# Merging the first loads of x in a matmul with bias and residual, and casting one tile on GpSimd

## The chip, the cores and the metric

The kernel runs on one core of one Trainium2 chip. The metric is device time in microseconds (us) of that core, lower being better. A core has five engines that run side by side[...]: PE (matmul, with PEld for its weight loads), DVE (VectorE), ACT (ScalarE), POOL (GpSimd) and SP, whose queue issues nearly all DMAs here. The profile also tells the share of the full TensorE clock that was granted at each moment (PEclk).

## The reference

```python
# x: (16, 512, 1024) f32, weight: (1024, 768) f32, bias: (768,) f32, residual: (16, 512, 768) f32
def reference(x, weight, bias, residual):
    return (np.matmul(x, weight) + bias + residual).astype(np.float32)
```

Flattened, x is 8192 rows of 1024 values and the output 8192 rows of 768.

## The kernel before, in words

**Tiling.** The 8192 rows are cut into 8 superblocks S of 1024 rows; partition p of a superblock holds 8 consecutive rows, so a superblock is `[128, J=8, 1024]`, and a tile t (64 in all) is the slice j = t % 8. A tile of x is 512 KB in f32. The contraction of 1024 is 8 steps of 128 (`steps`, c in 0..3 and e in 0..1); the output's 768 columns are two chunks, 512 and 256.

**What happens to a tile.** `cast(t)` converts x to bf16 into `xb[t]` (ring of 4). `transp(t)` views pairs of bf16 as f32, transposes four 128x128 blocks on PE into the PSUM tile `pt`, and DVE copies them to `xt[t]`. `mms(t, i)` runs the two chunks of one contraction step; 16 matmuls make a tile. `finish(t)` on DVE adds bias (tiles below 24) or the residual (later ones) to the PSUM result `po`, and `pool_add(t)` on POOL adds the rest. SP stores the result rows, which lie in the buffer that the residual was loaded to.

**Order.** Everything inside `keep_in_program_order` stays, on each engine, in the order in which the source issues it; nothing is planned by costs. SP's queue holds all loads and stores except the bias row, which ACT issues. The DMAs' completion semaphores are eight in rotation, so a DMA is issued only when the eighth one before it has landed.

**The head**, which the change touches, is written out by hand. SP issues, from first to last: tiles 0 and 1 of x as two DMAs (16 partitions, then the other 112), tile 2, the four blocks of weights `load_w(0..3)` of 768 KB each, then tile 3, tiles 4 and 5, tiles 6 and 7, and after these residual and x in turn. PE runs twelve dummy matmuls on a zeroed tile (`keep_warm(12)`), which keep it busy while nothing has landed, then the transposes of tiles 0 and 1, three more dummies, the transpose of tile 2, and a small matmul that spreads the bias row over the partitions (L193). Then the main matmuls start: for each weight block c, tiles 0, 1 and 2 in turn (`HEAD` = 3). DVE casts tile 0, ACT tiles 1 and 2; ACT and DVE cast the weights, half each, as the blocks land. From tile 3 on, one loop runs a tile per turn: the cast of tile t + 2 on ACT, sixteen matmuls with the transposes of tile t + 1 between them, `finish(t - 1)`. A buffer of x (two in a ring) is loaded again when all eight casts that read it are done.

The lines of the profile named below: L66 loads of x, L77 of weights, L74 of the residual; L89 the cast of x; L97 the transposes; L101 the copy to `xt`; L106 the main matmuls; L173 the dummies; L179 and L181 the casts of the weights; L193 and L201 the bias; L123 POOL's add.

Of the kernel before, what the change touches and what calls it, by code (L numbers as in the profile page):

```python
# [10 lines left out]
P = 128  # L11
J = 8
# [9 lines left out]
def kernel(  # L22
# [8 lines left out]
    nc = tc.nc  # L31
# [11 lines left out]
    x_d = x2d.rearrange("(S p j) k -> S p j k", p=P, j=J)  # L43
# [8 lines left out]
    def ring(pool, name, i, n, shape, dt):  # L52
        return pool.tile(shape, dt, name=name, tag=f"{name}{i % n}", bufs=1)
# [4 lines left out]
    x_sb, ro, xb, xt, po, tmp = {}, {}, {}, {}, {}, {}  # L58
    K_ = tc.keep_in_program_order


    def load_x(S, j0=0, j1=J, p0=0, p1=P):
        if S < n_s:
            if j0 == 0 and p0 == 0:
                x_sb[S] = ring(sb, "x_tile", S, X_BUFS, [P, J, K], FP32)
            K_(nc.sync.dma_start(  # L66
                out=x_sb[S][p0:p1, j0:j1, :], in_=x_d[S, p0:p1, j0:j1, :]
            ))

    def load_res(S, j0=0, j1=J):  # L70
        if S < n_s:
            if j0 == 0:
                ro[S] = ring(sb, "ro", S, RO_BUFS, [P, J, N], FP32)
            K_(nc.sync.dma_start(out=ro[S][:, j0:j1, :], in_=res_d[S, :, j0:j1, :]))  # L74

    def load_w(c):
        K_(nc.sync.dma_start(out=w_st[:, c, :, :], in_=w_d[:, c, :, :]))  # L77
# [7 lines left out]
    def cast(t, engine="act"):  # L85
        if t < n_t:
            xb[t] = ring(sb, "xb", t, 4, [P, K], BF16)
            copy = nc.scalar.copy if engine == "act" else nc.vector.tensor_copy
            K_(copy(out=xb[t], in_=x_sb[t // J][:, t % J, :]))  # L89

    def transp(t):
        if t < n_t:

            pt = ring(ps, "pt", t, 2, [P, n_c, P], FP32)
            pairs = xb[t][:, :].bitcast(FP32)
            for c in range(n_c):
                K_(nc.tensor.transpose(  # L97
                    out=pt[:, c, :], in_=pairs[:, c * P:(c + 1) * P], identity=ident
                ))
            xt[t] = ring(sb, "xt", t, 4, [P, n_c, P], FP32)  # L100
            K_(nc.vector.tensor_copy(out=xt[t], in_=pt))  # L101
# [37 lines left out]
    w_st = ring(sb, "ro", RO_BUFS - 1, RO_BUFS, [P, n_c, 2, N], FP32)  # L139
    w_sb = const.tile([P, n_c, 2, N], BF16, name="w_sb")  # L140

    load_x(0, 0, 2, 0, 16)
    load_x(0, 0, 2, 16, P)
    load_x(0, 2, 3)
    load_w(0)
    load_w(1)
    load_w(2)
    load_w(3)
    load_x(0, 3, 4)
    load_x(0, 4, 6)  # L150
    load_x(0, 6, 8)
    load_res(0, 0, 4)
    load_x(1, 0, 4)
    load_res(0, 4, 8)
# [16 lines left out]
    def keep_warm(n):  # L171
        for _ in range(n):
            K_(nc.tensor.matmul(  # L173
                warm_ps[:, 0:512], lhsT=warm[:, 0:P], rhs=warm, start=True, stop=True
            ))
# [5 lines left out]
            K_(nc.vector.tensor_copy(out=w_sb[:, c, e, :], in_=w_st[:, c, e, :]))  # L181


    keep_warm(12)
    cast(0, "dve")
    cast(1)
    transp(0)
    transp(1)
    keep_warm(3)
    cast(2)  # L190
    transp(2)
    for n0, nl in chunks:
        K_(nc.tensor.matmul(  # L193
# [23 lines left out]
    for t in range(HEAD, n_t):  # L217
        cast(t + 2)
        S, j = divmod(t, J)
# [30 lines left out]
    t, S = n_t - 1, n_s - 1  # L250
# [36 lines left out]
```

## Time and profile before

| | |
|---|---|
| median of 3 runs | 212.18 us (212.13 to 212.57) |
| the profiled execution | 212.57 us, of which the span from first to last instruction is 210.8 us and 1.8 us lie around it |
| PE busy | 201.7 us, 96% of the span |
| POOL, DVE, ACT busy | 115.7, 104.9 and 68.3 us |
| DMA | 87.23 MB, mean 414 GB/s |
| mean granted TensorE clock | 0.990 |

The page sums up one execution; the rows quoted below come from it and from four views of the same trace: the chain of work that ended last, in order of time; the timeline of an engine; the busy times and granted clock by stretch; and the DMA rates. In the chain, a piece is what the next piece waited for, and an engine's pieces follow each other without a gap. A matmul's modelled duration overlaps the next one's, so spacing between starts tells more than durations do.

### The profile page before, as it was taken

What the parts mean: (1) busy time and instruction counts of PE and PEld (TensorE: products, weight loads), DVE (VectorE), ACT (ScalarE), POOL (GpSimd) and SP (SyncE); (2) the same over time, 40 slices, a digit from 0 to 9 for tenths busy, and PEclk for the clock granted to TensorE, in tenths of its full rate; (3) what the DMA queues carried; (4) which work ended last, traced back from release to release, by engine and by line L of the source; (5) the groups of instructions that cost most, each with busy time, mean ns of one, the idle gap of its engine ahead of it and who ended that gap; (6) DMA issues with size and microseconds to landing.
All of it is one profiled execution on the core that took longest, in us unless ns stands there. A gap on an engine that the chain in (4) does not pass through costs nothing.

```text
span 210.8 us, 3154 instructions
## 1 busy us (share of the span) xinstructions
PE 201.7 (96%) x1274; PEld 131.8 (63%) x1299; DVE 104.9 (50%) x139; ACT 68.3 (32%) x68; POOL 115.7 (55%) x71
## 2 busy tenths in 40 slices
PE   7599999999999999999999999999999999999992
PEld 2366666666666666666666666666666666666651
DVE  0364554455445544554455455445544554455652
ACT  2443507240723142331333133321532333231000
POOL 2000077918865565799779901995059910699000
PEclk9889999999999999999999999999999999999999
DMA  6999999999999999999999999999999999999984
GB/s 170 373 414 426 443 403 443 454 395 438 432 454 421 420 438 404 463 431 412 428 443 431 424 415 429 452 426 426 438 423 432 442 417 423 434 438 421 423 373 182
DMA packets 5648, 87.23 MB, mean 414 GB/s; under 512 B 641, under 2 KB 769, under 8 KB 1922
## 3 DMA queue, kind: packets, MB, share of 16 engines
q1 hardware_dynamic: 5632, 87.03, 97.8%
q8 instruction: 10, 0.16, 0.3%
q14 instruction: 4, 0.03, 0.0%
q10 hardware_dynamic: 2, 0.00, 0.0%
HBM read 61.87 MB, written 25.17 MB: 413 GB/s over the span
## 4 chain that ended last, share of the span: by engine, by line
PE 93%; DMA 3%; DVE 1%; issue 1%; SPq 0%; DVEq 0%
PE po L106 78%; PE pt L97 14%; DMA x_tile<-in_x_dram 3%; PE po L193 1%; PE po L173 1%; DVE xb L89 0%; DVE xt L101 0%; DVE ro L133 0%; SPq L66 0%; DVEq L89 0%
## 5 line engine op out<-in xcount | busy, mean ns | idle before, releaser
L106 PE MATMUL po<-w_sb,xt 128*128 128x512 bf16 (+1 forms) x999 | 175.4, 324 | 1.4
L106 PEld LDWEIGHTS <-xt 128*128 128x128 bf16 x1024 | 100.1, 98 | 59.5 <-DVE xt L101 0.5
L89 ACT CAST xb<-x_tile 128x1024 bf16<-128x1024 f32 x62 | 63.5, 1045 | 117.5 <-PE pt L97 67.1
L123 POOL TENSOR_TENSOR ro<-ro,bias_sb 128x768 f32<-128x768 f32 x40 | 71.2, 1817 | 34.3 <-DMA ro<-in_residual_dram 23.0
L101 DVE COPY xt<-pt 128x512 f32<-128x512 f32 x64 | 44.3, 692 | 88.8 <-PE pt L97 88.7
L123 POOL TENSOR_TENSOR ro<-ro,tmp 128x768 f32<-128x768 f32 x24 | 43.2, 1817 | 44.5 <-DVE xt L101 25.6
L97 PE MATMUL pt<-ident,xb 128*128 128x128 f32 x256 | 39.3, 278 | 2.4 <-DVE xb L89 2.4
L133 DVE TENSOR_TENSOR ro<-po,ro 128x768 f32<-128x768 f32 (+2 forms) x41 | 38.0, 929 | 2.9 <-PE po L106 2.8
L97 PEld LDWEIGHTS pt<-ident,xb 128*128 128x128 f32 x256 | 30.8, 144 | 10.5 <-issue 3.3
L131 DVE TENSOR_TENSOR tmp<-po,bias_sb 128x768 f32<-128x768 f32 x24 | 22.8, 948 | 1.9 <-PE po L106 1.9
L173 PE MATMUL po<-warm 128*128 128x512 bf16 x15 | 6.2, 586 | 1.2 <-DVE warm L159 1.2
L89 DVE CAST xb<-x_tile 128x1024 bf16<-128x1024 f32 x2 | 1.4, 694 | 6.9 <-DMA x_tile<-in_x_dram 6.9
L173 PEld LDWEIGHTS <-warm 128*128 128x128 bf16 x15 | 2.0, 142 | 4.1 <-issue 2.8
L179 ACT CAST w_sb<-ro 128x768 bf16<-128x768 f32 x4 | 3.3, 832 | 4.0 <-DMA ro<-in_weight_dram 4.0
L181 DVE CAST w_sb<-ro 128x768 bf16<-128x768 f32 x4 | 2.1, 553 | 0.8 <-DMA ro<-in_weight_dram 0.8
L164 ACT ACT_TABLE_LOAD x1 | 1.3, 1283 | 2.0 <-POOL ident masks.py:199 2.0
L193 PE MATMUL po<-tmp 128*128 128x512 f32 (+1 forms) x4 | 1.5, 500 | 0.0
L193 PEld LDWEIGHTS po<-tmp 128*128 128x128 f32 x4 | 0.8, 240 | 0.5 <-issue 0.5
L201 DVE COPY bias_sb<-po 128x768 f32<-128x768 f32 x1 | 1.0, 958 | 0.1
L137 POOL MEMSET tmp<- 128x768 f32 x1 | 0.7, 737 | 0.3 <-POOLq L271 0.3
L159 DVE MEMSET warm<- 128x256 uint32 x1 | 0.3, 272 | 0.9 <-PEq L271 0.9
masks.py:199 POOL TENSOR_SCALAR_AFFINE_SELECT ident<-ident 128x128 f32<-128x128 f32 x1 | 0.3, 292 | 0.1
(8 smaller groups left out, 1.0 us busy)
## 6 DMA issues: line engine op xcount, KB each, us to landing
ro<-in_residual_dram SPq DMA_DIRECT2D x7, 3072.0 KB, 18.2
out_dram<-ro SPq DMA_DIRECT2D x7, 3072.0 KB, 24.0
x_tile<-in_x_dram SPq DMA_DIRECT2D x5, 4096.0 KB, 28.8
x_tile<-in_x_dram SPq DMA_DIRECT2D x4, 2048.0 KB, 26.5
ro<-in_weight_dram SPq DMA_DIRECT2D x4, 768.0 KB, 10.1
ro<-in_residual_dram SPq DMA_DIRECT2D x2, 1536.0 KB, 21.2
x_tile<-in_x_dram SPq DMA_DIRECT2D x2, 1024.0 KB, 15.0
out_dram<-ro SPq DMA_DIRECT2D x1, 1536.0 KB, 9.9
```

Of the source, the lines that this page charges most:

```text
L89: K_(copy(out=xb[t], in_=x_sb[t // J][:, t % J, :]))
L97: K_(nc.tensor.transpose(out=pt[:, c, :], in_=pairs[:, c * P:(c + 1) * P], identity=ident))
L101: K_(nc.vector.tensor_copy(out=xt[t], in_=pt))
L106: K_(nc.tensor.matmul(po[t][:, n0:n0 + nl], lhsT=both[:, e, :], rhs=w_sb[:, c, e, n0:n0 + nl], start=(i == 0), stop=(i == len(steps) - 1),))
L123: K_(nc.gpsimd.tensor_add(out=r, in0=r, in1=tmp[t] if t < EARLY else bias_sb))
L131: K_(nc.vector.tensor_add(out=tmp[t], in0=p, in1=bias_sb))
L133: K_(nc.vector.tensor_add(out=row(t, n0, nl), in0=p, in1=row(t, n0, nl)))
L164: K_(nc.scalar.copy(out=warm_a, in_=warm_a))
L173: K_(nc.tensor.matmul(warm_ps[:, 0:512], lhsT=warm[:, 0:P], rhs=warm, start=True, stop=True))
L179: K_(nc.scalar.copy(out=w_sb[:, c, e, :], in_=w_st[:, c, e, :]))
L181: K_(nc.vector.tensor_copy(out=w_sb[:, c, e, :], in_=w_st[:, c, e, :]))
L193: K_(nc.tensor.matmul(bias_ps[:, n0:n0 + nl], lhsT=ones, rhs=bias_row[:, n0:n0 + nl], start=True, stop=True,))
```

## The change

The first DMA of x takes all three tiles of the head, 1536 KB over 128 partitions; the loads after the weights take two tiles and three. Six DMAs of x become three. The cast of tile 2 moves from ACT to POOL. Two dummy matmuls move from between the transposes of tiles 1 and 2 to the stretch before the first transpose: 12 and 3 become 14 and 1.

```diff
-    def load_x(S, j0=0, j1=J, p0=0, p1=P):
+    def load_x(S, j0=0, j1=J):
         if S < n_s:
-            if j0 == 0 and p0 == 0:
+            if j0 == 0:
                 x_sb[S] = ring(sb, "x_tile", S, X_BUFS, [P, J, K], FP32)
-            K_(nc.sync.dma_start(
-                out=x_sb[S][p0:p1, j0:j1, :], in_=x_d[S, p0:p1, j0:j1, :]
-            ))
+            K_(nc.sync.dma_start(out=x_sb[S][:, j0:j1, :], in_=x_d[S, :, j0:j1, :]))
...
-            copy = nc.scalar.copy if engine == "act" else nc.vector.tensor_copy
+            copy = {
+                "act": nc.scalar.copy, "dve": nc.vector.tensor_copy,
+                "pool": nc.gpsimd.tensor_copy,
+            }[engine]
...
-    load_x(0, 0, 2, 0, 16)
-    load_x(0, 0, 2, 16, P)
-    load_x(0, 2, 3)
+    load_x(0, 0, 3)
     load_w(0)
     load_w(1)
     load_w(2)
     load_w(3)
-    load_x(0, 3, 4)
-    load_x(0, 4, 6)
-    load_x(0, 6, 8)
+    load_x(0, 3, 5)
+    load_x(0, 5, 8)
...
-    keep_warm(12)
+    keep_warm(14)
     cast(0, "dve")
     cast(1)
     transp(0)
     transp(1)
-    keep_warm(3)
-    cast(2)
+    keep_warm(1)
+    cast(2, "pool")
     transp(2)
```

## The prediction

> **What bounds the kernel now.** I read the chain of waits first, by engine for the whole page and then in order of time for the first 26 us, where all edits lie.
>
> ```profile
> PE 93%; DMA 3%; DVE 1%; issue 1%; SPq 0%; DVEq 0%
> ```
>
> ```profile
> 1.18 6.12 DMA x_tile<-in_x_dram
> ...
> 7.41 0.71 DVE xb L89
> 8.11 0.14 issue
> 8.25 1.68 PE pt L97 x8
> 9.92 1.28 PE po L173 x3
> 11.20 0.85 PE pt L97 x4
> 12.06 1.30 PE po L193 x4
> 13.36 2.93 PE po L106 x18
> ```
>
> PE sets the end, and from 13.2 us to 206.7 us it is busy without a gap over 0.14 us. So the change is worth what it moves the start of the main matmuls, unless it opens a later gap. Ahead of them stand the DMA that brings tiles 0 and 1 (landed 7.30), DVE's cast, then PE's work in order.
>
> Second view: busy time and granted clock by stretch (PE, PEld, DVE, ACT, POOL, then PEclk, DMA share, GB/s).
>
> ```profile
> 1.19:5.13 3.94, 3.94 (x10) 1.46 (x11) 0.08 (x2) 1.47 (x2) 0.71 (x3) 1.00 0.83 221
> 5.13:8.55 3.42, 1.05 (x7) 0.46 (x6) 0.69 (x1) 1.07 (x2) 0.00 (x0) 1.00 1.00 335
> 8.55:11.96 3.41, 3.41 (x15) 2.60 (x14) 1.38 (x2) 1.86 (x2) 0.00 (x0) 0.50 1.03 422
> 11.96:13.20 1.24, 1.24 (x6) 0.62 (x6) 1.11 (x2) 0.83 (x1) 0.00 (x0) 1.00 1.00 411
> ```
>
> From 8.55 to 11.96 PE runs at half clock. The stretch of equal length before it was only 31% busy (1.05 of 3.42), since PE idles from 5.88 to 8.25. Half clock explains 0.21 us a transpose (0.85 for 4) against about 0.11 later (0.60 for 4, drain included). The first dummies are also slow (weight loads 0.43 apart), though PEclk reads 1.00 there: no change of clock is recorded before.
>
> Third: the data's arrival, GB/s over the first 24 us in slices of 0.6 us, and the casts.
>
> ```profile
> GB/s 0 0 41 287 82 300 314 251 341 232 246 321 440 406 430 410 410 440 379 440 389 451 410 420 406 386 416 464 437 410 437 423 423 437 423 403 512 410 389 430
> ```
>
> ```profile
> 7.39 2.19 ACT L89 CAST xb<-x_tile 128x1024 bf16<-128x1024 f32 x2 [3.88 <-DMA x_tile<-in_x_dram]
> 7.41 0.69 DVE L89 CAST xb<-x_tile 128x1024 bf16<-128x1024 f32 x1 [6.13 <-DMA x_tile<-in_x_dram]
> ```
>
> ACT's second cast starts at 7.39 + 2.19 - 1.05 = 8.53, just after tile 2 landed (issued 1.64, 6.9 us to landing). From 7.2 us the DMAs run at full rate, and the weights land at 10.4, 12.3, 14.1 and 16.0.
>
> [...]
>
> **The change part by part.**
>
> *One load for three tiles.* Nothing can be cast before all three have landed. Same bytes in the same order, so about 8.5; the slice at 82 GB/s (2.4 to 3.0), between the first DMA and the second, may go, worth at most 0.6 us. But the 16-partition DMA may have been what started the engines early: I allow 0.3 us of loss. Landing between 7.9 and 8.8; I take 8.4, 1.1 us later than tiles 0 and 1 now. Transposes follow 0.94 later as now (7.31 to 8.25), so at 9.34.
>
> *Dummies 12/3 to 14/1.* The two before the transposes fall into PE's idle time: at 0.21 us each they end at about 6.3, cover 2.8 us of idleness more. They cost nothing, and delay nothing even if slow (0.85 us). The two taken out after the first transposes save 2 x 1.28/3 = 0.85 us at half clock.
>
> *Cast of tile 2 on POOL.* ACT is spared 1.05 us that nothing waited for. POOL's cast isn't in the trace. Below: POOL's memset of 768 columns took 0.74, so 1024 take 0.98[...]. Above: POOL's two-input add, 1.82 for 768, scaled to 2.42. I take 1.2. [...]PE needs it after eight transposes and a dummy: 9.34 + 1.70 + 0.43 = 11.47. Hidden, by 1.1 us at my value, and late by 0.1 at the upper end.[...] POOL has nothing else until 27.5 us.
>
> *Sum, with the clock restored at 11.96 as now.* At half clock: transposes 1.70, dummy 0.43, transposes 0.85, to 12.32. The last 0.36 lies past 11.96 and takes half: 12.14. Bias matmul 1.28 at full clock: main matmuls at 13.42. The same recipe for before: 8.25 to 8.55 does 0.60 of half-clock work, 3.23 is left of 3.83, so 11.78, and the bias ends at 13.15 (13.20 in the trace). Difference **+0.27 us**. Because this start moves by half of the landing, 7.9 gives +0.0 and 8.8 gives +0.5. The later arrival costs 1.1/2 = 0.55, the dummies give back about half of 0.6. I use +0.25.
>
> *What stands behind.* DVE copies `xt` of tile 2, then casts w0's half: about 12.3 to 13.5, needed at 13.7 (second step), so just hidden. Later weights are 1 us or more ahead.
>
> *Loads 3+2 in place of 1+2+2 after the weights.* Tile 3 lands with tile 4, 512 KB at 0.42 MB/us = 1.2 us later: 17.3 becomes 18.6, cast on DVE by 19.3, needed by PE at 20.5. Cover 1.1 us; DVE's `finish(0)` behind it is due at 20.2, so free. Tile 5 lands with 6 and 7 at 22.3, cast by 23.4, needed at 26.2. The last cast of buffer 0 ends at 25.5, not 24.4, so SP issues the next x loads 1.1 us later; 48.0 us is when the queue ahead of them drains, so nothing moves.
>
> *Three DMAs fewer on SP.* SP's issue ends earlier (three at 0.4 us), and residual and x loads are issued one place earlier in the rotation, since the eighth DMA before is an earlier one. They queue 16 us or more ahead of landing: no gain. Cost range of these edits: -0.1 to +0.1.
>
> The profiled execution took 212.57 (span 210.8 plus 1.8), 0.4 above the median of 212.18. I add the difference to the median: **212.4 us**.
>
> **Rivals.**
>
> 1. *The clock stays at full speed* (faster). Two more dummies fill the window before 8.55[...]. Against it: the window gains 0.43 of dummies but loses 0.30 of transposes, 1.05 now and about 1.2 then. For it: if transposes don't count, it gains 0.43. Then transposes 0.87, dummy 0.21, transposes 0.44 and bias 1.28, from 9.34: 12.2 with 0.1 for POOL. That is 1.0 earlier, less 0.2 waiting for tile 3's cast (needed at 19.3, done 19.3 plus wake-up). Time 211.4. Chance 0.16.
>
> 2. *The clock comes back a window later* (slower). PE starts at 9.34, so the window to 11.96 is 77% busy, and dummies alone are 0.43 of 3.41, 13% (now 38%). If that is too little, half clock lasts to 15.37. Work of 5.54 at half clock (1.70 + 0.43 + 0.85 + 2.56) ends at 14.9, another 0.24 is lost to 15.37: +1.9, time 214.1.[...] Chance 0.22.
>
> 3. *[...]* (slower). Both casts wait for one landing; DVE starts 0.10 after it, POOL 0.14 at its first add (27.39 landed, 27.53). [...]time 213.2. Chance 0.18, with landings after 8.8.
>
> 4. *Nothing moves*: tile 2 was needed anyway and the dummies pad to the same start: 212.2. It is the low end of my case.
>
> **How the numbers follow.** My case has 0.44, with its own range 212.1 to 212.8; of this some 0.37 lies within 0.2% (0.42 us, about what a measurement of this kernel can tell from no change) and 0.07 above. Slower: 0.07 + 0.22 + 0.18 = 0.47; faster 0.16. To hold 8 in 10 the range must reach both clock cases: 211.3 to 214.2.
>
> **What would show it.** Right: x lands once, near 8.4; the first transpose near 9.3; half clock from 8.55 to 11.96; main matmuls at 13.4; POOL's cast done before 11.4. A PEclk of 1.00 through 8.5 to 12 is rival 1, of 0.50 beyond 12 rival 2, DVE's cast a microsecond after the landing rival 3. Wrong altogether: a PE gap near 20 us for `transp(3)`, or the landing outside 7.9 to 8.8.

## The result, and the profile after

| | before | after |
|---|---|---|
| median, 6 runs each | 212.25 us (212.13 to 212.57) | 210.94 us (210.81 to 211.00) |
| ratio to before | 1 | 0.9937, 95% interval 0.9924 to 0.9949 |
| profiled execution, span | 212.57, 210.8 us | 210.81, 209.0 us |
| main matmuls start | 13.20 us | 11.03 us |
| last matmul ends | 206.7 us | 204.5 us |

The kernel became 1.3 us faster. I had forecast 212.4 and a range of 211.3 to 214.2, with slower as the likelier sign: the forecast was wrong. The main matmuls moved by 2.2 us, the time by only 1.3 (1.8 between the two profiled executions, which are the slowest of the six before and the fastest of the six after). That the time moved less turns out to matter.

The chain of waits of the changed kernel in order of time (start, duration, what):

```profile
0.74 6.16 DMA x_tile<-in_x_dram
...
6.92 0.71 DVE xb L90
7.63 0.14 issue
7.76 0.64 PE pt L98 x4
...
8.43 0.70 DVE xt L102
9.13 0.14 issue
9.27 0.63 PE pt L98 x4
9.89 1.29 PE po L191 x4
11.19 2.92 PE po L107 x18
```

All three tiles land at 6.90, before tiles 0 and 1 alone did (7.30), and 1.6 us before tile 2 did (8.51). The transposes take 0.11 us each in place of 0.21 (0.64 and 0.63 for four include the end of the last one). The clock by stretch says why; the columns are PE, PEld, DVE, ACT, POOL, PEclk, DMA share, GB/s:

```profile
5.13:8.55 3.42, 2.41 (x13) 1.25 (x12) 0.81 (x2) 1.04 (x1) 1.56 (x1) 1.00 0.99 418
8.55:11.96 3.41, 3.19 (x18) 1.83 (x17) 3.06 (x5) 1.67 (x2) 0.00 (x0) 1.00 1.00 418
```

PE idles only from 6.75 to 7.76, and no half clock follows. The last column of the first row is 418 GB/s, where it was 335. The DMA rate in slices of 0.6 us shows this from the start:

```profile
GB/s 0 0 102 225 164 430 369 410 471 435 328 420 420 420 440 430 410 410 440 440 410 430 430 437 437 423 492 430 389 471 430 348 492 430 389 430 471 410 403 437
```

Full rate is reached at 3.0 us in place of 7.2. From 3 to 7 us, before (first row) and after (second, its own trace):

```profile
3.00:7.00 4.00, 2.88 (x9) 0.88 (x7) 0.00 (x0) 0.50 (x2) 0.00 (x0) 1.00 0.96 278
```

```profile
3.00:7.00 4.00, 3.75 (x11) 1.18 (x9) 0.08 (x1) 0.58 (x3) 0.04 (x1) 1.00 0.97 408
```

The DMA share, 0.96 and 0.97, hides the difference: the DMA engines are as busy, only slower. Every later landing that can be matched lies earlier by 1.5 to 1.8 us: the loads of tiles 6 and 7 by 1.72 us (22.28 to 20.56), the residual of superblock 1 by 1.65 (48.00 to 46.35), the last store by 1.74 (209.82 to 208.08). That fits a queue that never runs empty, shifted as a whole.

### The profile page after: what moved, and what is told of

Same layout as the page of the kernel before. It is cut to its first block, busy times and chain, and to the rows that moved or that the text cites. A ratio compares the mean times of both kernels' runs of the same rounds, so it can differ in the third digit from the quotient of the medians.

```text
span 209.0 us, 3150 instructions
## 1 busy us (share of the span) xinstructions
PE 200.7 (96%) x1274; PEld 130.7 (62%) x1299; DVE 104.8 (50%) x139; ACT 67.2 (32%) x67; POOL 117.1 (56%) x72
## 3 DMA queue, kind: packets, MB, share of 16 engines
q1 hardware_dynamic: 5328, 87.03, 97.8%
## 4 chain that ended last, share of the span: by engine, by line
PE 93%; DMA 3%; DVE 1%; issue 1%
PE po L107 79%; PE pt L98 13%; DMA x_tile<-in_x_dram 3%; DVE xt L102 1%; PE po L191 1%; DVE xb L90 0%; DVE ro L134 0%
## 5 line engine op out<-in xcount | busy, mean ns | idle before, releaser
L90 ACT CAST xb<-x_tile 128x1024 bf16<-128x1024 f32 x61 | 62.4, 1045 | 116.4 <-PE pt L98 63.9
L98 PE MATMUL pt<-ident,xb 128*128 128x128 f32 x256 | 38.3, 273 | 1.2 <-DVE xb L90 1.0
L98 PEld LDWEIGHTS pt<-ident,xb 128*128 128x128 f32 x256 | 29.9, 141 | 9.3 <-issue 2.1
L90 POOL CAST xb<-x_tile 128x1024 bf16<-128x1024 f32 x1 | 1.6, 1557 | 5.0 <-DMA x_tile<-in_x_dram 5.0
```

What stands on the lines that cost most here:

```text
L98: K_(nc.tensor.transpose(out=pt[:, c, :], in_=pairs[:, c * P:(c + 1) * P], identity=ident))
```

## The experiments

Theory A: the old first load ran slowly because its two DMAs covered only part of the partitions, and a saturated DMA stream, not PE, sets the end. Its rivals: the length of the rows does it (8 KB then, 12 KB now); the dummies and the clock do it; POOL's cast does it; PE sets the end. The kernel before ran beside each group on the same chip (212.28, 212.38 and 212.56 us for the three groups below), so ratios to it compare better than times.

### Which of the edits does it

**The loads alone.**

```diff
-    load_x(0, 0, 2, 0, 16)
-    load_x(0, 0, 2, 16, P)
-    load_x(0, 2, 3)
+    load_x(0, 0, 3)
...
-    load_x(0, 3, 4)
-    load_x(0, 4, 6)
-    load_x(0, 6, 8)
+    load_x(0, 3, 5)
+    load_x(0, 5, 8)
```

> The three x loads of the change (3, 2 and 3 tiles), with the dummies left at 12 and 3 and tile 2 cast on ACT. Theory (the load's shape does it): tiles land near 6.9, PE idles from about 6.2 to 7.8 only (1.5 us), the clock stays at full, main matmuls start within 0.2 us of the changed kernel's 11.03, 211.0 us. Rival (the dummies hold the clock): with twelve dummies the idleness brings half clock back, main matmuls after 12, 212 us or more. Rival (POOL's cast matters): tile 2 waits for ACT's second cast until 9.0, a gap on PE, 211.2 us.

210.99 us, ratio 0.9938 (0.9926 to 0.9950); landing 6.81, main matmuls 10.96, full clock. The loads are the whole gain; neither the dummies nor POOL's cast is needed for it. (The run with tiles 0 and 1 in one DMA, below, narrows it to the first load alone.)

**The dummies alone.**

```diff
-    keep_warm(12)
+    keep_warm(14)
...
-    keep_warm(3)
+    keep_warm(1)
```

> The kernel before with the dummies 14 and 1, nothing else. Landings as before (7.3 and 8.5). If two more dummies shorten PE's idleness enough (6.3 to 8.25, 1.9 us) to keep full clock: main matmuls near 11.4 and 210.5 us. If half clock comes as before: only the two dummies at half clock are saved, less what the clock's return at a fixed time takes back, 0.4 us: 211.8 us.

212.27 us, ratio 0.9999 (0.9990 to 1.0008): nothing, though I had expected a gain in either case. Its profile is the most instructive of all:

```profile
8.55:11.96 3.41, 3.19 (x17) 1.86 (x16) 3.06 (x6) 1.51 (x3) 0.00 (x0) 1.00 1.01 414
```

The clock stays full, the main matmuls start at 10.81, 2.4 us before those of the kernel before, the last ends at 204.4; yet the last store lands at 209.75, against 209.82. 2.3 us of earlier PE changed nothing at the end: something else holds it. (In this execution the same loads landed 0.7 us earlier than in the profile before, at 6.61 and 7.74. The residual of superblock 1 still landed 0.45 earlier and the last load of x 0.39, that of the residual of superblock 7, next in the queue, only 0.1. Why the lead is lost there isn't settled.)

**POOL's cast alone.**

```diff
...
-    cast(2)
+    cast(2, "pool")
     transp(2)
```

> The kernel before with tile 2 cast on POOL, nothing else. Tile 2 lands over 0.4 us after DVE's cast of tile 0 ends[...]. If POOL's 1.56 us in the changed kernel held a wait of 0.66[...], it takes 0.9 here; if the two ran side by side, 1.56 again. Time: no change, 212.2 us, in either case.

212.48 us, ratio 1.0002 (0.9992 to 1.0011). POOL's timeline here, and then DVE's and POOL's rows of the changed kernel:

```profile
8.04 1.04 POOL L92 CAST xb<-x_tile 128x1024 bf16<-128x1024 f32 x1 [6.06 <-DMA x_tile<-in_x_dram]
```

```profile
6.92 0.69 DVE L90 CAST xb<-x_tile 128x1024 bf16<-128x1024 f32 x1 [5.65 <-DMA x_tile<-in_x_dram]
6.96 1.56 POOL L90 CAST xb<-x_tile 128x1024 bf16<-128x1024 f32 x1 [4.97 <-DMA x_tile<-in_x_dram]
```

Alone POOL takes 1.04; started 0.03 us after DVE's cast it takes 1.56, and DVE's own 0.69 is not stretched. The 0.52 more are most of the 0.66 for which DVE still ran. ACT's cast of tile 1 ran beside POOL's as well, and here it had just ended, but it is hardly the cause: all of POOL's 64 adds in the changed kernel take 1.81 to 1.83 us, though a cast of ACT lies beside 29 of them for over 0.5 us. What lengthens POOL's cast beside DVE's, and whether DVE's would be longer if POOL's had started first, no run shows. This kernel, too, ran its head at full clock in its profile (main matmuls near 11) and gained nothing.

### Why the old loads were slow

**Tiles 0 and 1 in one DMA, all else as before.**

```diff
-    load_x(0, 0, 2, 0, 16)
-    load_x(0, 0, 2, 16, P)
+    load_x(0, 0, 2)
```

> The kernel before with tiles 0 and 1 in one DMA over 128 partitions in place of 16 and 112; all else unchanged. Theory (a DMA over 112 partitions is slow, about 260 GB/s where 128 partitions move 420): tiles 0 and 1 land near 5.7, tile 2 near 7.0, full clock, main matmuls near 10.0 and 210.0 us, faster than the changed kernel. Rival (rows of 8 KB are slow at the start, rows of 12 KB are not): landing stays near 7.3, 212.2 us.

Tiles 0 and 1 land at 5.29, tile 2 at 6.67, main matmuls at 9.85: the landings are near those of the theory, and rows of 8 and 4 KB are not slow. The time is 211.07 us, ratio 0.9943 (0.9930 to 0.9955): taking this one cut away gives all of the gain that can be told, without tile 2 in the load or the merged later loads. But it is not 210.0: main matmuls 1.2 us earlier than in the changed kernel brought nothing. The residual of superblock 1 lands at 46.29, the changed kernel's at 46.35, and the last store is 5.0 us from issue to landing.

**The changed kernel with its first load cut at partition 16.**

```diff
...
-    load_x(0, 0, 3)
+    load_x(0, 0, 3, 0, 16)
+    load_x(0, 0, 3, 16, P)
```

> The changed kernel with its first load in two, 16 and 112 partitions, rows of 12 KB as in the change. Theory (112 partitions are slow): all three tiles land near 8.4, first transpose 9.3, about 212.3 us, most of the gain lost. Rival (row length is what counts): landing near 7.0, 211.0 us.

213.38 us, ratio 1.0061 (1.0040 to 1.0082). All three tiles land at 9.26, with rows of 12 KB. The rival of row length is out. The cut costs more than I expected: the landing is 0.9 us later than my 8.4, and 2.4 us later than in the changed kernel, which is also what the median lost. The profile shows the slowest of the six executions (214.62 us). In it half clock lasts to 16.27, the main matmuls start near 15.8, and PE's late start outweighs the stream: the last store needs only 1.9 us. The rate while the 112 partitions load, and the half clock after it:

```profile
5.00:9.00 4.00, 1.76 (x6) 0.55 (x4) 0.00 (x0) 0.00 (x0) 0.00 (x0) 1.00 0.94 271
9.50:15.00 5.50, 4.80 (x16) 3.49 (x17) 3.09 (x5) 2.63 (x4) 1.45 (x1) 0.50 1.02 419
```

**Cut into halves of 64 partitions.**

```diff
...
-    load_x(0, 0, 3)
+    load_x(0, 0, 3, 0, 64)
+    load_x(0, 0, 3, 64, P)
```

> The changed kernel with its first load in two halves of 64 partitions. Theory[...]: each half runs at about 200 GB/s, three tiles land near 10, time 213 to 215 us. Rival (only 112, not a multiple that fits 16 engines well, is slow): landing near 7.0, 211.0 us. Rival (it is the second DMA, whatever its shape, that starts late): landing near 7.5, 211.5 us.

215.44 us, ratio 1.0138 (1.0122 to 1.0154), a little over the expected range. The halves land at 7.04 and 10.76: 768 KB, 0.786 MB, in 3.72 us, 211 GB/s (the rate of the packets from 7 to 10 us is 180). The load over 112 partitions ran at 271 GB/s above, and the one over 128 in the changed kernel at 408 from 3 to 7 us. Why a load over fewer partitions is slower stays open. The packets show it too: one of 12 KB, a partition's row, takes 0.46 us (median) in the first load of the changed kernel, 0.73 with 112 partitions and 0.97 with 64.

**A later load cut at partition 16**, in the changed kernel: the residual of superblock 1, in the middle of the stream.

```diff
...
-    load_res(1)
+    load_res(1, 0, J, 0, 16)
+    load_res(1, 0, J, 16, P)
```

> The changed kernel with one later load split 16 + 112 partitions: the residual of superblock 1 (3072 KB, queued behind others from 12.5 us, landing near 46 us), where PE waits for nothing. Theory (the end hangs on the DMA stream[...]): 384 KB and 2688 KB take some 3.5 to 6 us more, every later landing moves by that, and so does the end: 214.5 to 217 us. Rival (the split costs only at the cold start): 211.0 us. Rival (PE is the bound, loads have slack): the landings move but the time stays at 211.0 us.

219.93 us, ratio 1.0350 (1.0331 to 1.0369): more than the 3.5 to 6 us that I had allowed. The stretches around it, of the changed kernel and then of this one:

```profile
36.00:46.00 10.00, 9.89 (x67) 6.75 (x68) 4.86 (x7) 3.99 (x4) 5.34 (x4) 1.00 1.00 424
46.00:56.00 10.00, 9.95 (x66) 6.53 (x66) 5.56 (x8) 3.97 (x4) 8.91 (x5) 1.00 1.04 442
```

```profile
36.00:46.00 10.00, 9.90 (x67) 6.75 (x68) 4.87 (x7) 3.08 (x4) 5.62 (x4) 1.00 1.02 225
46.00:56.00 10.00, 9.95 (x66) 6.42 (x65) 3.60 (x5) 0.81 (x1) 0.00 (x0) 1.00 1.00 292
56.00:66.00 10.00, 5.73 (x37) 3.56 (x37) 4.48 (x6) 4.24 (x5) 9.84 (x6) 1.00 1.01 432
```

The part of 16 partitions lands at 44.46, that of 112 at 56.01. Packets of both overlap with each other and with the next load's, so the rates of the stretches, 225 and 292 GB/s, say more than bytes by landing. The residual is complete 9.7 us later than in the changed kernel, and the program ends 9.5 us later in its profile (218.5 against 209.0). PE loses 4 us of work in the last stretch and makes up none of it, but it is not what ends last: its last matmul is done at 209.1, the last store lands at 217.6.

**The same load cut by rows**, 128 partitions in both DMAs, as a control.

```diff
-    load_res(1)
+    load_res(1, 0, 4)
+    load_res(1, 4, 8)
```

> The changed kernel with the residual of superblock 1 in two DMAs again, but cut by rows (4 and 4) with 128 partitions each. If the 9 us of the cut by partitions came from the shape of the DMAs: landing near 46.4 as in the changed kernel, 211.0 us. If any second DMA costs: over 212 us.

211.31 us, ratio 0.9940 (0.9920 to 0.9960), landing 46.73: a second DMA costs nothing that shows. The cut by partitions is what costs.

### What sets the end

**Five more dummies before the main matmuls**, in the changed kernel.

```diff
-    keep_warm(1)
+    keep_warm(6)
```

> The changed kernel with six dummies in place of one before the transpose of tile 2, which starts the main matmuls 5 x 0.216 = 1.1 us later at full clock, and touches no DMA of the stream's first part. Theory (the DMA stream sets the end): at most 0.3 us more, 210.9 to 211.2 us. Rival (PE sets the end, as I predicted from): 1.1 us more, 212.0 us.

211.40 us, ratio 0.9943 (0.9925 to 0.9961), against 0.9937 of the changed kernel; by these ratios 0.1 us more. In the profile the last matmul ends 0.65 us later, 205.19; the last store lands at 208.31 against 208.08. The delay is 0.65 and not 1.1 us because PE had waited there in any case, and the dummies fill that: in the changed kernel the one dummy starts at 8.67 and the transposes at 9.27, 0.38 us more than the 0.22 that a dummy takes. So this run tests little; the next one tests more.

**Six dummies fewer in the gap**, in the changed kernel, to bring half clock back with the loads untouched.

```diff
-    keep_warm(14)
+    keep_warm(8)
```

> The changed kernel with 8 dummies in place of 14 before the first transpose; loads untouched. PE then idles from about 4.6 to 7.8 us and half clock is likely in the head, with the main matmuls 1 to 2 us later. Theory (the DMA stream sets the end, PE has about 1 us to spare): 211.0 to 212.0 us, clearly less than the shift of the main matmuls. Rival (PE and its clock set the end): the whole shift, 212 to 213 us.

211.52 us, ratio 0.9952 (0.9934 to 0.9971), some 0.3 us more by the ratios, whose intervals overlap. The transposes run at half clock again, by their pace (1.94 us for eight; PEclk can't tell, since the first record of the clock in this trace comes at 12.82). The main matmuls start at 13.02 and the last ends at 206.5: both 2.0 us later and within 0.2 of the kernel before, which is 1.0 us slower than this one. This comparison separates the two halves of the change: with PE nearly as late as before and the loads of the change, about three quarters of the gain stays (0.48% of 0.63%). Here PE has used up what room it had: its last store takes 1.9 us from issue to landing, where the changed kernel's takes 3.1.

The view that I should have read is the time from issue to landing of the last store, 128 KB, for the kernel before, the changed one, the dummies alone and this one:

```profile
out_dram<-ro SPq DMA_DIRECT2D x1, 128.0 KB, 2.6
```

```profile
out_dram<-ro SPq DMA_DIRECT2D x1, 128.0 KB, 3.1
```

```profile
out_dram<-ro SPq DMA_DIRECT2D x1, 128.0 KB, 4.8
```

```profile
out_dram<-ro SPq DMA_DIRECT2D x1, 128.0 KB, 1.9
```

1.9 us is the shortest, and the changed kernel with its first load cut at 16, where PE is late too, shows the same; I take it as the time without a wait, an estimate. By it the store already waited 0.7 us in the kernel before, 1.2 in the changed one, 2.9 with PE made early. What PE gains, the store waits. The landings say the same: after the store of 768 KB has landed, the last 768 KB land in 1.91 us before (207.92 to 209.82) and in 1.90 after, 412 and 415 GB/s, so the stream runs at nearly its full rate to the end. With six dummies fewer they take 2.56 us, 308 GB/s, since PE hands them over too late.

## Why the prediction was wrong, point by point

Two steps failed: the path that sets the end, and the landing of the first load. The second gave the forecast its sign, the first its value.

**"PE sets the end", and the change is worth what it moves the start of the main matmuls.** The DMA stream sets it. The chain of waits shows PE in all of these kernels because it ends at DVE's last add (at 205.0 us in the changed kernel), three microseconds before the last store lands (208.1); the stores ahead of that one in the queue are not in it. With the measured start of 11.03 the same reckoning would have said 210.0; measured were 210.94. The profiled execution before was one in which both bounds nearly met: half clock had made PE late, and the last store took only 0.7 us more than the shortest, 1.9. Moving the main matmuls by 2.4 us earlier alone brought nothing (dummies alone), 2.0 us later cost about 0.3 (six dummies fewer). The signs were on the page: the last store's 2.6 us, and this line, the share of sixteen engines' time that the queue's packets took:

```profile
q1 hardware_dynamic: 5632, 87.03, 97.8%
```

**The landing, 7.9 to 8.8, taken as 8.4.** It was 6.9, outside the range, which the prediction itself names as a sign of being wrong altogether. "Same bytes in the same order" assumed that the rate was given. I explained the slice at 82 GB/s and not the seven after it at 232 to 341, in the line that I quoted. They were the time of the load over 112 partitions: 278 GB/s from 3 to 7 us. The 16-partition DMA, which I credited with perhaps starting the engines early, did not: the first packets start at 1.75 us in the one trace and at 1.74 in the other.

**The value of the loads.** Bytes under way from 3 to 7 us: (408 - 278) GB/s x 4 us = 0.52 MB, at 428 GB/s of the steady stream 1.2 us. From 7 to 15 us the rates were 419 and 427, another 0.15 us. That is most of the shift of 1.6 to 1.7 us in the head between the two profiles; the rest I can't place. Over all runs the medians differ by 1.3 us.

**Half clock from 8.55 to 11.96 as a fixture.** Of the kernels that kept the old loads, the dummies alone and POOL's cast alone had full clock through the head in their profiles, with the first landing 0.45 us or more earlier. So it is not fixed even for one head, and I had built the sum on its edges. In time it is worth little here: see six dummies fewer.

The prediction left open whether transposes help to keep the clock. Three kernels with the same twelve dummies, which end near 5.9 us, answer it: the kernel before, the loads alone and POOL's cast alone. In their traces the clock's first record comes at 5.13, 5.14 and 5.18 us, and in the kernel before the clock fell 3.41 us later, at 8.55; I compare that stretch in all three. Before, transposes filled 0.30 us of it, PE 1.05 in all, and half clock followed. In the other two an earlier landing let them fill 0.87 and 0.75, and full clock stayed (PE's busy time 1.62 and 1.53):

```profile
5.13:8.55 3.42, 1.62 (x12) 1.02 (x11) 0.90 (x2) 1.71 (x2) 0.00 (x0) 1.00 0.97 405
```

```profile
5.13:8.55 3.42, 1.53 (x11) 0.91 (x10) 0.78 (x2) 1.04 (x1) 0.51 (x1) 1.00 1.00 358
```

With the dummies alike, the transposes made the difference in PE's busy time. So in these three traces full clock went with more transposes, 0.75 and 0.87 us against 0.30, and it was the earlier data, not more dummies, that brought them. For rival 2 (how busy a stretch must be to bring full clock back) the changed kernel with its first load cut at 16 has a case: PE was busy for 2.66 us of the stretch from 9.45 to 12.86, mostly with transposes, and half clock went on; the next one, to 16.27, busy throughout, ended it.

**The dummies.** "About half of 0.6" given back, 0 in the run with the dummies alone. The two moved forward were not needed either: with 12 and 3 the gap grew to 1.8 us and the clock stayed.

**POOL's cast.** Right: DVE's cast was not held up (0.69 us, as before), and POOL took 1.04 by itself in place of my 1.2, done at 8.5 in the changed kernel, 0.7 us before PE used it. The 1.1 us that I forecast for this cover came from an end at 10.4 (8.4 + 0.1 + 0.69 + 1.2; 11.6 with the upper 2.42), with POOL's cast set whole behind DVE's, an assumption of mine; beside DVE's cast it took 1.56. Rival 3, DVE's cast late behind POOL's, was my assumption too, and did not occur.

**Later loads.** Right in kind: no stall at tile 3, although the cover was 0.47 us (cast done 17.60, transposes at 18.07), not 1.1.

**Rivals.** Rival 1, full clock, had 0.16. Its clock came true and so did its sign, with 211.4; but it put both down to the dummies and the clock, and in time the dummies alone do nothing. Its sign was luck. A rival with a faster first load, or with the DMA stream as the bound, was missing.

## What to carry to other kernels

Where the DMA queue is nearly full from start to end (97.8% here), ask first whether the last store waited (time from issue to landing, against the shortest in these traces: 2.6 us against 1.9 here). Here it had, and main matmuls 2.4 us earlier left the time as it was (ratio 0.9999), while a faster first load gave 0.9943. Compare the rate of each load with that of the steady state: a busy share near 1 goes with 278 GB/s here as well as with 408. Try a cut by rows before one by partitions: in the middle of this stream the cut at partition 16 took the ratio from 0.9937 to 1.0350, the cut by rows, with all 128 partitions in every DMA, to 0.9940.

## What the runs showed of the hardware that I had not expected

- While a load over 64 partitions (64 to 127) was under way in the head the stream moved 211 GB/s by its landings (180 by its packets from 7 to 10 us), with one over 112 (16 to 127) 271 to 278 in the head and 292 in mid-stream, where loads over 128 moved 408 in the head of the changed kernel and 424 to 442 in mid-stream; one such cut of 3 MB cost 9 us of 211.
- The load cut by partitions in mid-stream held back what was queued behind it on the same queue to the end of the program: 9.7 us at its landing were 9.5 us at the end.
- POOL's cast of 128x1024 from f32 to bf16 took 1.04 us alone, near ACT's 1.045, and 1.56 beside a DVE cast that had started 0.03 us before.
- At full clock, a stretch of 3.41 us with 1.05 us of PE work (the kernel before) was followed by half clock, and ones with 1.53 (POOL's cast alone) and 1.62 (the loads alone) were not, transposes counted. At half clock, 2.66 us (first load cut at 16) did not bring full clock back, and 3.41 (the kernel before, 8.55 to 11.96) did.
